# Two-layer encoder on one core: conditioning vector loaded as eight rows, inputs loaded first, layer 0's rotary tables made by TensorE

## The chip, the cores and the metric

One core of one Trainium2 chip. The kernel is written in Bass; its own planner simulates five engines (TensorE as PE, VectorE as DVE, ScalarE as ACT, GpSimd as POOL, and SyncE as SP, which issues every load) and writes the instructions in the order that the simulation gave. The metric is the device time of one launch in microseconds, lower is better.

## The reference

A two-layer encoder over 256 tokens of width 1024. Each layer has a mixer (grouped-query attention with normed and rotated queries and keys, a dilated windowed attention, gates) and a squared-ReLU MLP of width 4096. Both are preceded by an RMS norm that is scaled and shifted by numbers made from a vector c:

```python
c_act = jax.nn.silu(c)
for l in range(DEPTH):
    ada = c_act @ w_ada[l] + b_ada[l]
    sh1, sc1, gt1, sh2, sc2, gt2 = [a[:, None, :] for a in jnp.split(ada, 6, axis=-1)]
    h = rms(x, g_mix[l]) * (1.0 + sc1) + sh1
    parts = jnp.split(h @ w_in[l], IN_SPLITS, axis=-1)
    qa = axial_rope(rms(qa, q_norm_a[l]), row_cs, col_cs)      # likewise k, and apply_rope for branch B
    ...
    x = x + gt1 * (mixed @ w_out[l])
    h2 = rms(x, g_mlp[l]) * (1.0 + sc2) + sh2
    x = x + gt2 * (jnp.square(jax.nn.relu(h2 @ w_ff1[l])) @ w_ff2[l])
```

All arrays are fp32; every weight is read once, so 6 x 1024 x 1024 weights a layer go into `ada` alone.

## The kernel before, in words

**Precision and weights.** A product of fp32 matrices is made of three fp32r matmuls (`mm3`): both operands are split into a rounded part and the rest. A weight piece is a tile of 128 x 1024 (512 KB), loaded into one of six raw buffers (`wr`). ACT writes its rounded part and DVE the rest (`split_next`); the pair is called `w`. The activations are kept as such a pair too, `hT`.

**The dot products with c.** `ada` is no matmul: for each output block of 128 the transposed piece of w_ada is loaded into a raw buffer as well, and one DVE instruction multiplies it by c_act, which stands on all 128 partitions, and sums along the row (`ada_tile`). 96 such pieces cover both layers. The results of a norm are `shg` (shift and scale); `sh_sc` adds the bias and the norm's weights.

**The beginning.** SP loads c spread over 128 partitions (512 KB, of which each row is the same 4 KB), the two halves of x (each 128 tokens, 512 KB), the identity and the small tile. ACT and DVE make silu of c on the whole 128 x 1024 tile. For each half of x, ACT sums the squares (`sum_sq`), POOL takes the power -1/2, DVE scales, PE transposes against the identity, and ACT copies the result into `xT` (`rms_x`).

**The loop of layer 0's first projection.** Eight k steps. Each needs two pieces of w_ada (shift and scale for this block of 128), their small instructions (`sh_sc`), then h = xT times scale plus shift on ACT twice (once in fp32, once rounded into `hT`), the rest on DVE, and two weight pieces, w_x and w_y, of four chunks by two token halves: 24 matmuls of 512 columns into eight accumulators that fill all PSUM banks. So a step takes in four loads of 512 KB, and on DVE two dot products, two weight rests, one rest of hT and the factors.

**The rotary tables.** `rope_tables(l)` loads the constants (`cst`, 256 KB, once) and the norm weights of the heads spread over 128 partitions (`gains`, twice 256 KB), ACT multiplies half of the gains by 8, and POOL multiplies gains and cosines or sines, eight instructions. For layer 0 it is recorded at k step 3, for layer 1 at the end of layer 0's MLP. The tables are used by `qk_post`, after the loop.

**What sets the order.** `Plan.due` gives each instruction a due time, worked back from PE's sequence; `Plan.run` starts, on each engine, the ready instruction that is due first and whose buffers are free. All instructions are then issued from line 492, so the profile knows them by that line and by their tiles. SP issues loads strictly in its order: a load whose raw buffer is still being read holds up all loads behind it. The eight DMA semaphores go round, so a load also waits for the one eight places ahead of it.

## Time and profile before

| | us |
|---|---|
| median of three runs | 770.52 (769.89 to 770.74) |
| profiled execution | 770.36 |
| its span | 768.6 |
| PE busy | 736.4 (96%) |
| DVE busy | 583.3 (76%) |
| ACT busy | 445.4 (58%) |
| POOL busy | 104.4 (14%) |

The page gives, for each engine, busy time, share of the span and number of instructions. In an order of time each row has its start, its duration, engine, line, operation, output and inputs, and in brackets the idle time before it and what ended it. Several like instructions may be drawn together in a row (x24). In the views, `shg` are the factors of a norm, `ss` the sums of squares, `s2k` a scratch tile, `ps` a PSUM bank, `tabs` the rotary tables.

### The profile page before, as it was taken

To read this page: it belongs to the slowest core of one execution; us is meant where nothing else is said; L and a number is where in the kernel's file an instruction comes from. 1 tells how busy PE (TensorE), PEld (TensorE's weight loads), DVE (VectorE), ACT (ScalarE), POOL (GpSimd) and SP (SyncE) were. 2 spreads that over 40 slices of the span, in tenths; PEclk is the share of its full clock that TensorE was granted. 3 is DMA by queue.
4 is the path that set the end of the run, shared out by engine and by line. 5 is a ranking of instruction groups with operands and counts; after the bars stand their busy time and mean duration, and the time that the engine had idled before them with its cause. 6 is when DMAs were issued, how large, how long until landed. Compare 5 with 4: busy or idle time off the path is not lost.

```text
span 768.6 us, 12113 instructions
## 1 busy us (share of the span) xinstructions
PE 736.4 (96%) x4632; PEld 646.9 (84%) x4632; DVE 583.3 (76%) x846; ACT 445.4 (58%) x693; POOL 104.4 (14%) x88
## 2 busy tenths in 40 slices
PE   3899999999999999999999999999999999999997
PEld 2678787899778999988878888889987999988896
DVE  5899999998899989755387999855789975445512
ACT  6459549995246665555344655697734775545520
POOL 1307840000000006000013744000000000000000
PEclk9999999999999999999999999999999999999999
DMA  9895677895559999985423697943553996666201
GB/s 340 320 390 215 203 275 259 320 328 206 164 177 406 385 402 344 341 289 182 132 94 103 228 316 254 337 149 110 184 173 111 382 375 229 191 193 190 84 1 55
DMA packets 50666, 181.30 MB, mean 236 GB/s; under 512 B 5648, under 2 KB 5936, under 8 KB 50608
## 3 DMA queue, kind: packets, MB, share of 16 engines
q1 hardware_dynamic: 50608, 180.53, 66.6%
q8 instruction: 36, 0.59, 0.3%
q14 instruction: 22, 0.18, 0.1%
HBM read 179.44 MB, written 1.06 MB: 235 GB/s over the span
## 4 chain that ended last, share of the span: by engine, by line
PE 70%; DVE 19%; issue 5%; DMA 2%; ACT 2%; POOL 1%; SPq 0%; POOLq 0%; DVEq 0%
PE ps L492 70%; DVE s2k L492 10%; DVE w L492 6%; DMA ident<-in_ident 1%; DVE rstd L492 1%; DMA wr<-in_w_ada 1%; DVE hT L492 1%; ACT pr L492 1%; POOL ss L492 1%; DVE x L492 1%; DMA wr<-in_w_gate 1%; ACT w L492 1%; DVE st L492 0%; ACT s2k L492 0%; SPq L492 0%
## 5 line engine op out<-in xcount | busy, mean ns | idle before, releaser
L492 DVE TENSOR_TENSOR w<-wr,w 128x1024 fp32r<-128x1024 f32 x236 | 289.2, 1247 | 73.9 <-ACT w L492 73.3
L492 ACT ACTIVATE w<-wr 128x1024 fp32r<-128x1024 f32 x236 | 245.6, 1057 | 120.0 <-PE ps L492 57.9
L492 PE MATMUL ps<-hT,w 128*128 128x256 f32 x2112 | 270.4, 285 | 0.3 <-DVE w L492 0.3
L492 PEld LDWEIGHTS ps<-hT,w 128*128 128x128 f32 x2112 | 260.1, 191 | 7.0 <-issue 3.6
L492 PE MATMUL ps<-w,r2k 128*128 128x512 f32 x768 | 178.7, 392 | 0.0
L492 PEld LDWEIGHTS ps<-w,r2k 128*128 128x128 f32 x768 | 143.2, 188 | 30.5
L492 PE MATMUL ps<-w,hT 128*128 128x512 f32 x672 | 162.1, 395 | 5.4 <-ACT hT L492 3.6
L492 PEld LDWEIGHTS ps<-w,hT 128*128 128x128 f32 x672 | 123.8, 188 | 33.9 <-ACT hT L492 5.7
L492 DVE CUSTOM_DVE_ANT_0 s2k<-wr,c_act 128x1024 bf16<-128x1024 f32 x96 | 118.7, 1254 | 7.8 <-DMA wr<-in_w_ada 7.5
L492 ACT ACTIVATE s2k<-ps 128x512 f32<-128x512 f32 (+2 forms) x108 | 56.7, 558 | 69.5 <-PE ps L492 68.8
L492 POOL TENSOR_TENSOR ss<-ss,half 128x1 f32<-128x1 f32 x8 | 8.3, 1035 | 315.7 <-DVE ss L492 315.7
L492 POOL TENSOR_TENSOR s2k<-s2k,tabs 128x256 f32<-128x256 f32 (+1 forms) x40 | 39.5, 1009 | 84.7 <-DVE w L492 36.3
L492 DVE TENSOR_TENSOR r2k<-s2k,r2k 128x512 fp32r<-128x512 f32 x28 | 19.3, 689 | 36.5 <-ACT r2k L492 36.5
L492 PE MATMUL ps<-w,mT 128*128 128x512 f32 x192 | 44.5, 391 | 0.0
L492 PE MATMUL ps<-ident,s2k 128*128 128x128 f32 x148 | 23.7, 294 | 19.8 <-DMA ident<-in_ident 12.0
L492 PEld LDWEIGHTS ps<-w,mT 128*128 128x128 f32 x192 | 35.8, 188 | 7.3
L492 PEld LDWEIGHTS ps<-ident,s2k 128*128 128x128 f32 x148 | 18.0, 149 | 26.7 <-issue 13.4
L492 POOL TENSOR_TENSOR rstd<-rstd,half 128x8 f32<-128x8 f32 (+1 forms) x20 | 37.2, 1872 | 3.4 <-DVE rstd L492 3.1
L492 ACT ACTIVATE pr<-pr,st 128x256 f32<-128x256 f32 (+1 forms) x64 | 35.9, 614 | 1.8 <-DVE st L492 1.7
L492 ACT ACTIVATE s2k<-x 128x512 bf16<-128x512 f32 x16 | 10.0, 626 | 41.6 <-DVE x L492 41.6
L492 POOL TENSOR_TENSOR tabs<-s2k,cst 128x384 f32<-128x384 f32 (+1 forms) x16 | 19.9, 1281 | 76.8 <-ACT s2k L492 76.8
L492 DVE TENSOR_TENSOR s2k<-ps,gtb 128x512 f32<-128x512 f32 x16 | 11.0, 686 | 24.3 <-PE ps L492 24.3
(68 smaller groups left out, 472.7 us busy)
## 6 DMA issues: line engine op xcount, KB each, us to landing
wr<-in_w_ff SPq DMA_DIRECT2D x120, 512.0 KB, 5.0
wr<-in_w_ada SPq DMA_DIRECT2D x96, 512.0 KB, 5.1
wr<-in_w_gate SPq DMA_DIRECT2D x32, 512.0 KB, 5.1
wr<-in_w_qkv SPq DMA_DIRECT2D x24, 512.0 KB, 4.3
wr<-in_w_x SPq DMA_DIRECT2D x16, 512.0 KB, 4.4
wr<-in_w_out SPq DMA_DIRECT2D x16, 512.0 KB, 5.0
wr<-in_w_y SPq DMA_DIRECT2D x8, 512.0 KB, 5.5
wr<-in_w_ba SPq DMA_DIRECT2D x8, 512.0 KB, 4.5
```

Source lines behind the costliest of these rows:

```text
L492: getattr(self.real[o["e"]], o["op"])(*map(real, o["a"]), **{n: real(z) for n, z in o["k"].items()})
```

## The change

1. **c.** c is loaded as a tile of 8 x 128. ACT takes tanh of it, DVE one instruction (tanh + 1) * c, so that the tile holds twice the silu; the dot products are scaled by 0.5. PE then spreads the eight rows over 128 partitions: eight fp32 matmuls, each with one column of the identity, repeated 128 times, as the stationary operand over 8 rows. ACT copies the two banks into c_act.
2. **Loads first.** Loads recorded under `plan.first()` get a due time ahead of everything: c, x's first half, identity, x's second half, the small tile.
3. **Warm-up.** Three fp32 matmuls of a zeroed 128 x 512 tile into a bank that nobody reads stand at PE's beginning.
4. **Sum of squares.** That of x's second half in layer 0's first norm goes from ACT to DVE.
5. **Layer 0's tables.** The cosines and sines come transposed (`cs_t`, 64 head columns by 256 tokens, 256 KB), the norm weights of the heads as eight columns of the small tile. DVE makes, for both halves of the partitions, an identity of 64 times each of the eight columns (`diag`); a matmul over 64 rows then gives cos times gain in one go: per token half four matmuls (128 and 384 columns, cosines in the upper 64 rows of the array, sines in the lower), and ACT copies the two banks into the tables. POOL and the spread gains are out of layer 0. `cst` is loaded in `rope_tables`, now only for layer 1.
6. **The planner.** A price for fp32 matmuls of more than 256 columns over 128 rows, and caching that leaves its rules as they were.

```diff
+    def first(self):
+        self.soon = True
+        yield
+        self.soon = False
...
+            if o["soon"]:
+                due[i] = i - 1e9
...
-        dve.tensor_tensor_reduce(junk, raw, c_act, 1.0, 0.0, ALU.mult, ALU.add, col)
+        dve.tensor_tensor_reduce(junk, raw, c_act, 0.5, 0.0, ALU.mult, ALU.add, col)
...
-        if CFG["dve_ss"]:
+        if (l, w, t) == (0, 0, 1):
             dve.tensor_tensor_reduce(junk, xc, xc, 1.0 / D, 0.0, ALU.mult, ALU.add, o)
...
+    def first_tables():
+        tabs = tl("sbuf", [P, 2, 2, 8, HD], F32, "b8", NB8, "tabs0")
+        cs = s2k("cs").rearrange("p (o n) -> p o n", o=2)
+        sp.dma_start(cs, a["cs_t"])
+        gc = small[:, 128:136]
+        dve.tensor_scalar(gc[:, 1::2], gc[:, 1::2], 8.0, None, op0=ALU.mult)
+        e = s2k("eye")[:, :HD]
+        dve.tensor_tensor(e, ident[:, 0:HD], ident[:, HD:P], op=ALU.add)
+        dg = s2k("diag")
+        dve.tensor_tensor(
+            dg.rearrange("p (s n) -> p s n", s=8), e[:, None, :].to_broadcast([P, 8, HD]),
+            gc[:, :, None].to_broadcast([P, 8, HD]), op=ALU.mult,
+        )
+        for t in range(2):
+            pss = [pt(f"tab{t}{hf}") for hf in range(2)]
+            with plan.together():
+                for o, (s0, s1) in enumerate(((0, 2), (2, 8))):
+                    for hf in range(2):
+                        rows = slice(HD * hf, HD * (hf + 1))
+                        pe.matmul(
+                            pss[hf][:, s0 * HD : s1 * HD], cs[rows, o, t * P : (t + 1) * P],
+                            dg[rows, s0 * HD : s1 * HD], start=True, stop=True,
+                        )
+            for hf in range(2):
+                act.activation(tabs[:, t, hf], pss[hf].rearrange("p (s n) -> p s n", s=8), AF.Copy)
+        return tabs
...
     def rope_tables(l):
+        sp.dma_start(cst, a["cst"])
...
-    sp.dma_start(c_act, a["c"].partition_broadcast(P))
-    for t in range(2):
-        sp.dma_start(x[:, t, :], a["x"][t])
-    sp.dma_start(ident, a["ident"])
-    sp.dma_start(small, a["small"])
-    c_sig = tl("sbuf", [P, 2 * D], F32, "b8", NB8, "c_sig")[:, :D]
-    act.activation(c_sig, c_act, AF.Tanh, scale=0.5)
-    act.activation(c_sig, c_sig, AF.Copy, scale=0.5, bias=0.5)
-    dve.tensor_tensor(c_act, c_act, c_sig, op=ALU.mult)
+    c_row = cp.tile([KT, P], F32, name="c_row")
+    with plan.first():
+        sp.dma_start(c_row, a["c"])
+        for t in range(2):
+            sp.dma_start(x[:, t, :], a["x"][t])
+            if t == 0:
+                sp.dma_start(ident, a["ident"])
+        sp.dma_start(small, a["small"])
+    c_sig = s2k("c_sig")[:KT, :P]
+    act.activation(c_sig, c_row, AF.Tanh, scale=0.5)
+    dve.scalar_tensor_tensor(c_row, c_sig, 1.0, c_row, op0=ALU.add, op1=ALU.mult)
+    warm = tl("sbuf", [P, 2 * D], F32, "b8", NB8, "warm")[:, :512]
+    dve.memset(warm, 0.0)
+    cold = tl("psum", [P, 512], F32, "ps", 8, "cold")
+    for _ in range(WARM):
+        pe.matmul(cold, warm[:, :P], warm, start=True, stop=True)
+    for g in range(2):
+        ps = pt(f"c{g}")
+        for k in range(4):
+            kk = 4 * g + k
+            pe.matmul(
+                ps[:, k * P : (k + 1) * P], ident[:KT, kk : kk + 1].to_broadcast([KT, P]), c_row,
+                start=True, stop=True,
+            )
+        act.activation(c_act[:, g * 512 : (g + 1) * 512], ps, AF.Copy)
...
+    tabs_of[0] = first_tables()
     hT = h_tiles(0, 0)
...
         if k == 3:
-            sp.dma_start(cst, a["cst"])
             sp.dma_start(mask, a["mask"])
-            tabs_of[0] = rope_tables(0)
```

**How the instructions move.** The beginning differs, the loop, and a few places of the qk post-processing behind it; from there on the engines run through the same rows, but for the late load of `cst` and one weight rest on DVE. First SP at the beginning of the program, before and now (`wr` are the raw buffers):

```order
L492 DMA c_act<-in_c 128x1024
L492 DMA x<-in_x 128x1024 x2
L492 DMA wr_99<-in_w_ada 128x1024
L492 DMA wr_100<-in_w_ada 128x1024
L492 DMA wr_101<-in_w_x 128x1024
L492 DMA ident<-in_ident 128x128
L492 DMA small<-in_small 128x128
L492 DMA wr_102<-in_w_y 128x1024
L492 DMA wr_103<-in_w_ada 128x1024
L492 DMA wr_104<-in_w_ada 128x1024
L492 DMA s2k_79<-in_gains 128x512
L492 DMA cst<-in_cst 128x512
```

```order
L523 DMA c_row<-in_c 8x128
L523 DMA x<-in_x 128x1024
L523 DMA ident<-in_ident 128x128
L523 DMA x<-in_x 128x1024
L523 DMA small<-in_small 128x136
L523 DMA wr_101<-in_w_ada 128x1024
L523 DMA wr_102<-in_w_ada 128x1024
L523 DMA s2k_74<-in_cs_t 128x512
L523 DMA wr_103<-in_w_x 128x1024
L523 DMA wr_104<-in_w_y 128x1024
L523 DMA wr_105<-in_w_ada 128x1024
L523 DMA wr_106<-in_w_ada 128x1024
```

x, the identity and the small tile stand ahead of all weights; the spread c, both gains and `cst` are gone from here, `cs_t` is new.

Then DVE at its beginning, before, and now from its sums of squares of x's second half to the first dot product with c (an ISA row with `wr` and `c_act` is a dot product, one with `x` a sum of squares, one without inputs reads out the sum; `small` holds the gains):

```order
L492 MEMSET half 128x16
L492 TENSOR_TENSOR c_act<-c_act,c_sig 128x1024
L492 SCALAR_TENSOR_TENSOR ss_75<-ss_75 128x1
L492 ISA s2k_85,shg_96<-wr_99,c_act 128x1024
L492 ISA shg_96 128x1
L492 TENSOR_SCALAR s2k_81<-x,ss_75 128x512
L492 ISA s2k_82,shg_96<-wr_100,c_act 128x1024
L492 ISA shg_96 128x1
```

```order
L523 ISA s2k_79,ss_92<-x 128x512
L523 ISA ss_92 128x1
L523 ISA s2k_80,ss_92<-x 128x512
L523 ISA ss_92 128x1
L523 TENSOR_SCALAR s2k_75<-x,ss_91 128x512
L523 SCALAR_TENSOR_TENSOR ss_92<-ss_92 128x1
L523 TENSOR_SCALAR s2k_76<-x,ss_91 128x512
L523 TENSOR_SCALAR small<-small 128x4
L523 TENSOR_TENSOR s2k_78<-s2k_77,small 128x512
L523 TENSOR_SCALAR s2k_79<-x,ss_92 128x512
L523 TENSOR_SCALAR s2k_80<-x,ss_92 128x512
L523 ISA s2k_75,shg_98<-wr_101,c_act 128x1024
```

The first dot product stood fourth and stands seventeenth now, behind two sums of squares, the four scalings of x, the scaling of small and the diagonal (`s2k_78`). Last, DVE between step 0's rest of `hT` and step 1's, before and now (`w` are the weights' rests, read from a raw buffer):

```order
L492 TENSOR_TENSOR hT_95<-s2k_82,hT_94 128x256
L492 ISA s2k_81,shg_96<-wr_103,c_act 128x1024
L492 ISA shg_96 128x1
L492 ISA s2k_83,shg_96<-wr_104,c_act 128x1024
L492 ISA shg_96 128x1
L492 TENSOR_TENSOR shg_96<-shg_96,small 128x2
L492 SCALAR_TENSOR_TENSOR shg_96<-shg_96,small 128x1
L492 TENSOR_TENSOR w_107<-wr_99,w_107 128x1024
L492 TENSOR_TENSOR hT_95<-s2k_84,hT_94 128x256
```

```order
L523 TENSOR_TENSOR hT_97<-s2k_76,hT_96 128x256
L523 ISA s2k_79,shg_98<-wr_105,c_act 128x1024
L523 ISA shg_98 128x1
L523 TENSOR_TENSOR w_108<-wr_104,w_108 128x1024
L523 ISA s2k_80,shg_98<-wr_106,c_act 128x1024
L523 ISA shg_98 128x1
L523 TENSOR_TENSOR shg_98<-shg_98,small 128x2
L523 SCALAR_TENSOR_TENSOR shg_98<-shg_98,small 128x1
L523 TENSOR_TENSOR w_109<-wr_101,w_109 128x1024
L523 TENSOR_TENSOR w_110<-wr_102,w_110 128x1024
L523 TENSOR_TENSOR hT_97<-s2k_75,hT_96 128x256
```

The second weight rest of step 0 (`w_108` now) and both of step 1 stand between the two rests of `hT` now, where one weight rest stood. On ACT the four copies into the tables stand behind step 0's two weight pieces and ahead of step 1's. On PE the three warm-ups, the eight matmuls that spread c, the sixteen transposes and the eight matmuls of the tables stand ahead of step 0, in this order.

More of the change, by code (lines that the diff above doesn't have):

```diff
@@ L2 @@
 from contextlib import ExitStack, contextmanager, nullcontext
+from functools import lru_cache
 import ml_dtypes
@@ L40 @@
 NB8 = 14
+WARM = 3
 QA, KA, VA, B0, GA = 0, 512, 640, 768, 3072
@@ L162, in together @@
     @contextmanager
+    def first(self):
+        self.soon = True
+        yield
+        self.soon = False
+    @contextmanager
     def together(self):
@@ L180, in foot, with blocks @@
         p0, at = divmod(x.offset, row)
+        return name, str(x.space), p0, p0 + parts, Plan.blocks(at, tuple(map(tuple, dims[1:])), size, row)
+    @staticmethod
+    @lru_cache(None)
+    def blocks(at, dims, size, row):
         idx = np.array([at])
-        for step, n in dims[1:]:
+        for step, n in dims:
             if step:
@@ L188, in foot @@
             m |= 1 << b
-        return name, str(x.space), p0, p0 + parts, m
+        return m
     def record(self, e, op, a, k):
@@ L197, in record @@
         o = dict(e=e, op=op, a=a, k=k, w=[self.foot(z) for z in outs], r=[self.foot(z) for z in ins], i=len(self.ops))
-        o["also"], o["then"] = [], None
+        o["also"], o["then"], o["soon"] = [], None, self.soon and e == "SP"
         if self.group is not None:
@@ L214, in cost @@
             if op == "matmul" and F32R not in (ins[0].dtype, ins[1].dtype):
+                if n > 256 and ins[0].ap[0][1] == P:
+                    return 1.7 * n, 1.7 * n + 220.0
                 return 1.0 * n, n + 220.0
@@ L349, in run @@
         then = dict.fromkeys(ORDERED)
+        state = [0]
+        seen = dict.fromkeys(ORDERED)
         def fits(i):
             more = {}
-            for name in sorted((z for z in names_of[i] if z not in begun), key=lambda z: place[z]):
+            new = [z for z in names_of[i] if z not in begun]
+            if not new:
+                return True
+            for name in sorted(new, key=lambda z: place[z]):
                 tag = self.tiles[name]
@@ L386, in run @@
                     heapq.heappush(q, (due[i], i))
+                    seen[e] = None
+                if pick is None and seen[e] == state[0]:
+                    continue
                 held = []
@@ L396, in run @@
                         break
+                if pick is None:
+                    seen[e] = state[0]
                 if pick is not None and e != "SP" and not forced:
@@ L432, in run @@
                     live[tag] += 1
+                    state[0] += 1
                     begun.add(name)
@@ L453, in run @@
                         if not users[name]:
+                            state[0] += 1
                             live[self.tiles[name]] -= 1
@@ L527, in encoder @@
     x = cp.tile([P, 2, D], F32, name="x")
-    small = cp.tile([P, 96 + 32], F32, name="small")
+    small = cp.tile([P, 96 + 32 + 8], F32, name="small")
     c_act = cp.tile([P, D], F32, name="c_act")
@@ L1264, in _constants @@
     mask = np.where(np.stack(rows, 1), 0.0, NEG).astype(ml_dtypes.bfloat16)
-    return cst, mask, np.eye(P, dtype=np.float32)
+    cs_t = np.ascontiguousarray(cst.transpose(3, 4, 2, 1, 0)).reshape(P, 2, S)
+    return cst, cs_t, mask, np.eye(P, dtype=np.float32)
 def _layout(i):
@@ L1273, in _layout @@
     r["x"] = con(f["x"].reshape(16, 4, 4, D).transpose(2, 1, 0, 3)).reshape(2, P, D)
-    r["c"] = f["c"].reshape(D)
+    r["c"] = f["c"].reshape(KT, P)
     b = f["b_ada"].reshape(2, 2, 3, KT, P)
@@ L1277, in _layout @@
     g = np.stack([f["g_mix"], f["g_mlp"]], 1).reshape(2, 2, KT, P).transpose(3, 0, 1, 2).reshape(P, 32)
-    r["small"] = con(np.concatenate([b_col, g], 1))
     r["w_ada"] = con(f["w_ada"].transpose(0, 2, 1)).reshape(2, 2, 3, KT, P, D)
@@ L1285, in _layout @@
     r["gains"] = con(np.stack([gains, sw], 1).reshape(2, 2, 512))
+    g0 = r["gains"][0].reshape(2, 8, HD).transpose(0, 2, 1).reshape(P, 8)
+    r["small"] = con(np.concatenate([b_col, g, g0], 1))
     cc = _chunk_cols()
@@ L1304, in _layout @@
     r["w_ff2"] = con(f["w_ff2"].reshape(2, 32, P, 1024))
-    r["cst"], r["mask"], r["ident"] = _constants()
+    r["cst"], r["cs_t"], r["mask"], r["ident"] = _constants()
     return r
```

## Prediction

> **What bounds the kernel now.** I read the page first, then who TensorE (PE) waits for, then PE's own order of time, then the engines that feed it, at the start. On the page:
>
> ```profile
> span 768.6 us, 12113 instructions
> PE 736.4 (96%) x4632; PEld 646.9 (84%) x4632; DVE 583.3 (76%) x846; ACT 445.4 (58%) x693; POOL 104.4 (14%) x88
> ```
>
> PE is busy for 736.4 of 768.6 us, so the change can win only from the 32 us in which it is not. PE's waits over the whole span:
>
> ```profile
> PE ps L492 <- DMA ident<-in_ident: 12.0, 1, 12.0
> PE ps L492 <- DVE s2k L492: 7.2, 10, 1.8
> PE ps L492 <- ACT hT L492: 3.6, 5, 1.2
> ```
>
> The 12.0 us lie ahead of PE's first instruction; the 3.6 lie in layer 0's first projection, eight k steps of 24 matmuls. PE in order of time:
>
> ```profile
> 12.02 3.65 PE L492 MATMUL ps<-ident,s2k 128*128 128x128 f32 x16 [12.02 <-DMA ident<-in_ident]
> 16.62 5.76 PE L492 MATMUL ps<-w,hT 128*128 128x512 f32 x24 [0.96 <-ACT hT L492]
> 23.56 1.19 PE L492 MATMUL ps<-w,hT 128*128 128x512 f32 x4 [1.18 <-ACT hT L492]
> 25.49 4.83 PE L492 MATMUL ps<-w,hT 128*128 128x512 f32 x20 [0.74 <-DVE hT L492]
> 30.70 5.76 PE L492 MATMUL ps<-w,hT 128*128 128x512 f32 x24 [0.37 <-ACT hT L492]
> 36.66 5.74 PE L492 MATMUL ps<-w,hT 128*128 128x512 f32 x24 [0.20 <-ACT hT L492]
> 43.28 22.08 PE L492 MATMUL ps<-w,hT 128*128 128x512 f32 x96 [0.89 <-ACT hT L492]
> 65.20 0.99 PE L492 MATMUL ps<-hT,w 128*128 128x256 f32 x7
> ```
>
> From step 4 on PE runs without a gap: 96 matmuls from 43.28 to 65.20, 0.228 us each, **5.48 us a step**. Eight such steps are 43.8 us; the loop takes 65.20 - 16.62 = 48.6. So 4.8 us are lost inside it, nearly all in steps 1 to 3, and 16.62 before it. The end of this loop, 65.20, is the number that the change must move. What made step 1 late is on VectorE (DVE) and GpSimd (POOL):
>
> ```profile
> 12.69 0.16 DVE L492 SCALAR_TENSOR_TENSOR shg<-shg,small 128x1 f32<-128x1 f32 x1
> 16.95 1.22 DVE L492 CUSTOM_DVE_ANT_0 s2k<-wr,c_act 128x1024 bf16<-128x1024 f32 x1
> 18.09 2.03 DVE L492 CUSTOM_DVE_ANT_0 s2k<-wr,c_act 128x1024 bf16<-128x1024 f32 x1
> 21.05 0.38 DVE L492 SCALAR_TENSOR_TENSOR shg<-shg,small 128x1 f32<-128x1 f32 x1
> 23.05 1.79 DVE L492 TENSOR_TENSOR w<-wr,w 128x1024 fp32r<-128x1024 f32 x1 [1.62 <-ACT w L492]
> 17.92 7.83 POOL L492 TENSOR_TENSOR tabs<-s2k,cst 128x384 f32<-128x384 f32 x8 [4.92 <-ACT s2k L492]
> ```
>
> While POOL builds the rotary tables (17.92 to 25.75), the same DVE instruction takes 2.03 us instead of 1.22, and a one-column one 0.38 instead of 0.16. Undisturbed, DVE's long instructions follow each other by 1.14 us (16.95 to 18.09).
>
> **Part by part: the start.** ScalarE (ACT), DMA and DVE up to step 0, with two later rows of DVE:
>
> ```profile
> 0.74 0.39 SPq L492 DMA_DIRECT2D c_act<-in_c  x1
> 1.18 0.89 SPq L492 DMA_DIRECT2D x<-in_x  x2
> 5.30 1.06 ACT L492 ACTIVATE c_sig<-c_act 128x1024 f32<-128x1024 f32 x1 [3.29 <-DMA c_act<-in_c]
> 14.85 0.60 ACT L492 ACTIVATE xT<-ps 128x512 f32<-128x512 f32 x1 [0.16 <-PE ps L492]
> 15.48 0.60 ACT L492 ACTIVATE s2k<-xT,shg 128x256 f32<-128x256 f32 x1
> 15.99 0.58 ACT L492 ACTIVATE hT<-xT,shg 128x256 fp32r<-128x256 f32 x1
> DMA to landing us min/median/max: 5.5/5.9/6.3
> 0.81 0.07 DVE L492 MEMSET half<- 128x16 f32 x1 [0.81 <-PEq L1313]
> 7.47 1.22 DVE L492 TENSOR_TENSOR c_act<-c_act,c_sig 128x1024 f32<-128x1024 f32 x1 [6.59 <-ACT c_sig L492]
> 13.04 0.88 DVE L492 TENSOR_SCALAR s2k<-x,ss 128x512 f32<-128x512 f32 x2 [0.18 <-POOL ss L492]
> 47.80 0.42 DVE L492 TENSOR_TENSOR hT<-s2k,hT 128x256 fp32r<-128x256 f32 x1
> 53.25 0.43 DVE L492 TENSOR_TENSOR hT<-s2k,hT 128x256 fp32r<-128x256 f32 x1
> ```
>
> Step 0's factors were ready on DVE at 12.69 + 0.16 = 12.85, yet ACT used them at 15.48: its queue stood behind the copies of the transposes, and these behind the identity. That cover goes; what is late next is DVE's chain:
>
> - Loads. The first 512 KB (c) were usable at 5.30, 4.6 us after issue; x's halves landed 5.5 and 6.3 us after their issues at 1.18 and about 1.6, so at 6.7 and 7.9. Now x's first half is the first big load: 5.3 at the latest (if the slow beginning is the queue's, not c's), 4.3 if it runs as x did. One 512 KB load costs 1.25 us (7.9 - 6.7), the identity's 64 KB an eighth. I take 5.3: identity 5.5, x's second half 6.7.
> - DVE, from 6.7: two sums of squares of 512 columns (half of 1.14 each) 1.2; four scalings of x, 0.44 each, 1.8; the diagonal, a 512-column instruction, 0.6; small ones 0.3; two dot products 2.3; the factors 0.4. That ends at **13.3**, 0.45 later than before: DVE got some 2.5 us of new work in front (sums of squares, diagonal, memset, identity's halves) and lost the 1.22 of c's product. POOL's power for x's second half (its row waits 0.18 for it above) lies beside a scaling and the diagonal. Without a row for the sums of squares' short form I bound them by 0.44 each (a scaling) and 0.7 (over half of 1.22): 13.0 to 13.5.
> - c comes off this path: it is spread by eight fp32 matmuls of 128 columns (0.22 each by the row below, 0.43 at half clock: 1.7 to 3.4 us) after the identity and the warm-ups, and two ACT copies of 0.6; over between 8.5 and 11, and DVE reads it at 10.6. ACT gives up two passes over c (1.06 each) and two squares.
> - PE's tables stand in front of step 0. fp32 prices and the full clock:
>
> ```profile
> 78.02 0.60 PE L492 MATMUL ps<-ident,s2k 128*128 128x128 f32 x4
> 111.73 1.13 PE L492 MATMUL ps<-ka,qk 64*128 64x256 f32 x8
> L492 PE MATMUL ps<-ident,s2k x148: 270/273/445, 12.0 to 597.0; 128*128 128x128 f32 x148
> ```
>
> One matmul lasts 0.27 us, overlapping the next. Four transposes take 0.60, so they start 0.11 apart; the first 16 took 3.65, 0.21 apart: half rate. The second row is four fp32 products of 64 rows, two by two in the halves of the array: (1.13 - 0.27) / 2 = 0.43 per pair of 256 columns, so 0.22 per pair of 128 and 0.65 per pair of 384: 1.7 us for all eight table matmuls if they run side by side, 3.5 if not. Transposes end near 11.5 (x's last scaling 10.6), tables at 13.2 or 15.0. I take 13.2, since their operands lie in the same halves as that row's. The warm-ups (three fp32 products of 512 columns: 2.6 us at full rate, 5.1 at half) run from about 1.5, behind DVE's memset that starts where the one at 0.81 did, while only loads are under way.
> - So ACT starts step 0's h at 13.3, and PE at 13.3 + (16.62 - 15.48) = **14.45**, where it was 16.62: 2.2 earlier. The other end, tables not side by side, is 15.0.
>
> **The loop.** Between its step-0 and step-1 rests of hT, DVE now has five long instructions (three weight rests, two dot products). A step with four took 53.25 - 47.80 = 5.45, so 0.89 of it is short work (factors, hT's rest of about 0.35), and five make 6.6. The step-0 rest ends at 13.3 + 1.14 + 0.35 = 14.8, so step 1's at 21.4. PE ends step 0 at 19.9, has 0.7 us of matmuls that need only the rounded part, and so step 1 counts from 20.7 and ends at 26.2; before, step 2 began at 30.70. POOL's 7.83 us are gone, ACT pays four copies of tables (0.6 each) after step 0's weights, before step 1's, and they end by 17.5, ahead of PE's need of those banks. Step 2's rest needs three long instructions, 4.3: 25.7. Later steps cost DVE 5.45 at most, less than PE's 5.48, so from 26.2 PE sets the pace: six steps, **59.1 against 65.20: 6.1 us**.
>
> The loads have to keep up:
>
> ```profile
> 16.60:23.50 6.90, 5.76 (x24) 4.43 (x24) 5.21 (x8) 3.69 (x8) 5.58 (x6) 1.00 1.03 419
> 23.50:30.70 7.20, 6.03 (x25) 4.35 (x25) 7.12 (x11) 4.17 (x6) 2.25 (x3) 1.00 0.71 241
> 48.00:54.00 6.00, 6.00 (x28) 4.99 (x27) 5.91 (x11) 3.66 (x5) 0.00 (x0) 1.00 1.02 406
> 280.00:290.00 10.00, 10.00 (x55) 8.63 (x55) 7.62 (x10) 4.90 (x8) 2.14 (x2) 1.00 1.03 394
> ```
>
> (Columns: window, length, PE, PEld, DVE, ACT, POOL busy, clock, DMA share, GB/s.) A step eats four loads, 2.1 MB in 5.48 us: 383 GB/s, under the 419 and 406 shown. Up to the last weights of the loop 18.5 MB go: 44 us at 419, from about 2 on; they land near 47.5 and are needed at 56. The Trainium skill (DMA: Bandwidth & Descriptors, Specifications) puts a core's HBM limit at about 358 GB/s; by that the last weights land near 55, are split by 57.2, and the loop ends near 60, a gain of 5.2. The rows, above 358 for windows on end, contradict it.
>
> The rotary constants, 256 KB, are now loaded a second time, in a stretch where DMA is full (the last row). PE has no gap there, and weights are split well ahead; I cost it at nothing, and at 0.65 us (256 KB at 394 GB/s) if the cover failed.
>
> Behind the loop the same instructions follow in nearly the same order, so the shift stays: 768.6 - 6.1 = 762.5 of span. The profiled execution took 770.36, 1.8 more than its span and 0.16 below the median of 770.52. Forecast: **764.4**.
>
> **Rivals.** (1) The load buffers' turn stays the limit in steps 2 and 3, as the 241 GB/s window suggests: a load goes out only when DVE has read an old one. Those steps then take the 5.96 and 6.62 of before (30.70, 36.66, 43.28), 1.6 more than forecast: 766.0. Against it: the window lies right behind POOL's disturbance. 16%. (2) PE's clock falls back between the spread of c and step 0, where only transposes keep it awake for some 3 us; step 0 then begins at half rate, and 3.4 us at half rate cost 1.7: 766.1. Against it: after nothing but 16 transposes, step 0 took 5.76 at 16.62, as step 2 did at 30.70, so transposes had raised the clock. The Trainium skill (TensorE: Matmul & The Clock Gate, PE-mode transpose) states the rule of this rival, that transposes don't count as PE activity; the trace disagrees. 10%. (3) More: DVE, no longer held up, runs further ahead of PE by the loop's end than the 0.6 of before, and of PE's waits for it behind the loop (the longest 1.8) up to 1.5 goes: 762.9. Against it: the load buffers tie it to PE. 12%. (4) Nothing: the post-processing behind the loop is DVE's and takes back what PE won: 770.5. Against it: that work can begin only when the loop's banks are done, so it moves along. 3%. (5) Slower: PE stays at half clock through all that now stands ahead of step 0, because zeros and 8-row products don't wake it. Warm-ups 5.1, c 3.4, transposes 3.4, tables 6.9: from 1.5 to 20.3; step 0 at half rate 10.3, ending at 30.6, and seven steps more end at 69.0, 3.8 behind: 774.3. It decides if the clock is still half at about 26. Against it: the before's 3.65 us of transposes were enough. 4%.
>
> **The numbers.** The forecast's case has 55%; its own range is 763.3 (x lands 1 us sooner) to 765.6 (tables not side by side, cover of the late load gone). With rivals 1 to 3 that is 93%, and the range 762.3 to 767.0 holds all four with some room beside their prices. A measurement tells 0.2% (1.5 us) from no change: faster 0.93, same 0.03, slower 0.04.
>
> **What would show it.** Right: PE's first transposes near 8 to 9, step 0 near 14.5, DVE's dot products at 1.2 us throughout, PE gapless from about 26, the 256-column matmuls beginning near 59. Wrong: matmuls of step 0 at twice their time (2, 5); DVE waiting on DMA in steps 2 to 4 (1); x's second half later than 7.5; a loop end near 59 with a span above 766, which would mean the gain is given back behind it.

## The result and the profile after

The changed kernel takes **765.22 us** (median of four runs, 764.64 to 766.63) against 770.20 us for the kernel before beside it (769.69 to 770.74): a ratio of 0.9938, interval 0.9921 to 0.9955, or 5.0 us. The profiled execution took 765.02 us with a span of 763.2, 5.4 less than the 768.6 of before. The forecast was 764.4.

The page of the changed kernel, with the same columns as before:

```profile
span 763.2 us, 12186 instructions
PE 744.3 (98%) x4670; PEld 651.8 (85%) x4670; DVE 583.7 (76%) x854; ACT 443.8 (58%) x692; POOL 92.8 (12%) x80
```

TensorE is busy 7.9 us longer (warm-ups, spread, tables), though the whole is shorter. Whom TensorE waits for (total, times, longest):

```profile
PE ps L523 <- DVE s2k L523: 9.3, 12, 1.8
```

The 12.0 us for the identity and the 3.6 for `hT` are gone; the waits for VectorE's `s2k` have grown from 7.2 to 9.3. TensorE in order of time:

```profile
6.87 2.29 PE L523 MATMUL ps<-c_row,ident 8*128 8x128 f32 x16
9.08 1.09 PE L523 MATMUL ps<-ident,s2k 128*128 128x128 f32 x8
10.45 1.67 PE L523 MATMUL ps<-ident,s2k 128*128 128x128 f32 x8 [0.28 <-DVE s2k L523]
12.05 3.05 PE L523 MATMUL ps<-s2k,s2k 64*128 64x128 f32 x16
15.03 44.36 PE L523 MATMUL ps<-w,hT 128*128 128x512 f32 x192
59.23 0.51 PE L523 MATMUL ps<-hT,w 128*128 128x256 f32 x3
61.34 0.30 PE L523 MATMUL ps<-ident,s2k 128*128 128x128 f32 x1 [1.61 <-DVE s2k L523]
```

Step 0 begins at 15.03 (before: 16.62), all 192 matmuls of the loop run as one block, and it ends at 59.23 (65.20). The first 128 x 128 transposes behind the loop, those of the keys, wait 1.61 us for VectorE where they waited 0.31 before (66.50):

```profile
66.50 0.30 PE L492 MATMUL ps<-ident,s2k 128*128 128x128 f32 x1 [0.31 <-DVE s2k L492]
```

VectorE at the start and in step 3, and its last rest of `hT`:

```profile
7.02 0.69 DVE L523 CUSTOM_DVE_ANT_0 s2k<-x 128x512 bf16<-128x512 f32 x1 [1.11 <-DMA x<-in_x]
9.30 0.69 DVE L523 TENSOR_TENSOR s2k<-s2k,small 128x512 f32<-128x512 f32 x1
10.71 1.22 DVE L523 CUSTOM_DVE_ANT_0 s2k<-wr,c_act 128x1024 bf16<-128x1024 f32 x1
13.31 0.16 DVE L523 SCALAR_TENSOR_TENSOR shg<-shg,small 128x1 f32<-128x1 f32 x1
14.69 0.43 DVE L523 TENSOR_TENSOR hT<-s2k,hT 128x256 fp32r<-128x256 f32 x1
...
30.38 1.23 DVE L523 TENSOR_TENSOR w<-wr,w 128x1024 fp32r<-128x1024 f32 x1 [0.74 <-ACT w L523]
...
53.27 0.43 DVE L523 TENSOR_TENSOR hT<-s2k,hT 128x256 fp32r<-128x256 f32 x1
```

From its first dot product at 10.71 VectorE has hardly a gap up to step 7's rest at 53.27; the largest is the 0.74 in step 3, where a weight landed late. Before, its rests of step 0 and step 7 were:

```profile
16.60 0.43 DVE L492 TENSOR_TENSOR hT<-s2k,hT 128x256 fp32r<-128x256 f32 x1 [0.42 <-ACT hT L492]
58.65 0.43 DVE L492 TENSOR_TENSOR hT<-s2k,hT 128x256 fp32r<-128x256 f32 x1
```

### The profile page after: what moved, and what is told of

Read it like the earlier page. It is cut to its first block, busy times and chain, and to the rows that moved or that the text cites. A ratio compares the mean times of both kernels' runs of the same rounds, so it can differ in the third digit from the quotient of the medians.

```text
span 763.2 us, 12186 instructions
## 1 busy us (share of the span) xinstructions
PE 744.3 (98%) x4670; PEld 651.8 (85%) x4670; DVE 583.7 (76%) x854; ACT 443.8 (58%) x692; POOL 92.8 (12%) x80
## 4 chain that ended last, share of the span: by engine, by line
PE 70%; DVE 19%; issue 5%; DMA 2%; ACT 2%; POOL 1%; POOLq 0%; SPq 0%; DVEq 0%; ACTq 0%
PE ps L523 70%; DVE s2k L523 9%; DVE w L523 6%; DVE rstd L523 1%; DMA wr<-in_w_x 1%; DMA wr<-in_w_gate 1%; ACT pr L523 1%; POOL ss L523 1%; DMA x<-in_x 1%; DVE x L523 1%; ACT w L523 1%; DVE hT L523 1%; ACT s2k L523 0%; DVE st L523 0%; DVE shg L523 0%
## 5 line engine op out<-in xcount | busy, mean ns | idle before, releaser
L523 ACT ACTIVATE qk<-ps 128x512 f32<-128x512 f32 x16 | 9.6, 598 | 29.9 <-PE ps L523 29.9
```

Source lines behind the costliest of these rows:

```text
L523: getattr(self.real[o["e"]], o["op"])(*map(real, o["a"]), **{n: real(z) for n, z in o["k"].items()})
```

## The experiments

The theory at this point had two halves: VectorE, freed of GpSimd, feeds TensorE sooner; and TensorE's earlier loop end carries through. The rival was that the earlier start alone, or the clock, did it. In each expectation the letters mean what it says there. In the diffs `...` stands for lines left out, among them those that keep the planner's order where the text says that it is kept. All kernels were timed against the kernel before in the same batch (769.62, 769.97, 770.15 and 770.09 us in the four batches). The table has the marks that turned out to matter, from each kernel's profile (one execution), and the median and ratio of all its runs. A ratio's interval reaches 0.0009 to 0.0017 (about 1 us) to either side, so smaller differences between two kernels are not told apart by their totals:

| run | PE step 0 | DVE rest, step 0 | DVE rest, step 7 | key transposes | span | span less step-7 rest | median | ratio to before, interval |
|---|---|---|---|---|---|---|---|---|
| before | 16.62 | 16.60 | 58.65 | 66.50 | 768.6 | 710.0 | 770.20 | |
| changed | 15.03 | 14.69 | 53.27 | 61.34 | 763.2 | 709.9 | 765.22 | 0.9938 (0.9921 to 0.9955) |
| changed again | 14.76 | 14.74 | 52.52 | 60.60 | 762.2 | 709.7 | 765.67 | 0.9940 (0.9927 to 0.9953) |
| tables on GpSimd | 16.09 | 16.06 | 58.11 | 66.19 | 769.1 | 711.0 | 772.01 | 1.0037 (1.0023 to 1.0051) |
| only the tables | 17.10 | 17.08 | 56.19 | 64.27 | 765.8 | 709.6 | 767.63 | 0.9971 (0.9962 to 0.9981) |
| squares on ScalarE | 16.50 | 15.88 | 53.86 | 61.94 | 764.1 | 710.2 | 766.43 | 0.9957 (0.9944 to 0.9969) |
| later transposes | 14.88 | 14.54 | 52.61 | 61.15 | 762.2 | 709.6 | 764.49 | 0.9937 (0.9924 to 0.9949) |
| no warm-up | 14.54 | 14.52 | 53.01 | 61.10 | 762.4 | 709.4 | 764.87 | 0.9939 (0.9925 to 0.9952) |
| spread of 128 rows | 14.93 | 14.91 | 52.79 | 60.87 | 762.5 | 709.7 | 764.89 | 0.9934 (0.9922 to 0.9946) |
| GpSimd beside | 15.49 | 15.47 | 60.22 | 68.31 | 771.1 | 710.9 | 771.09 | 1.0013 (1.0004 to 1.0022) |
| TensorE later | 16.71 | 14.95 | 53.35 | 61.62 | 764.0 | 710.7 | 765.56 | 0.9941 (0.9929 to 0.9954) |
| VectorE later | 14.98 | 14.96 | 54.50 | 62.58 | 766.3 | 711.8 | 766.00 | 0.9951 (0.9939 to 0.9964) |
| shorter VectorE chain | 16.80 | 16.78 | 56.42 | 64.50 | 766.9 | 710.5 | 766.82 | 0.9954 (0.9941 to 0.9968) |
| mask later | 15.45 | 15.12 | 53.18 | 61.25 | 762.9 | 709.7 | 764.97 | 0.9941 (0.9926 to 0.9956) |

**The two halves of the change apart.** First the changed kernel with layer 0's tables back on GpSimd:

```diff
-    tabs_of[0] = first_tables()
...
         if k == 3:
+            tabs_of[0] = rope_tables(0)
```

> Layer 0's tables go back to POOL with their three 256 KB loads; c as eight rows, loads first, warm-ups and the squares on DVE stay. Theory A (the gain is the lead that DVE wins in the loop, and POOL's tables took 2.8 us of it): DVE's dot products and weight rests of steps 1 and 2 reach 1.5 to 2.0 us again, step 7's rest of hT comes 2 to 3 us later than in the changed kernel (53.3), time 767.2 to 768.2. Rival B (the loads and the early start of step 0 make the gain, POOL is hidden): step 0 at 14 to 14.5, since tables and diagonal are gone from in front of it, time 764.5 to 765.5.

Both numbers missed: at 772.01 it is slower than the kernel before. Its TensorE:

```profile
12.30 2.82 PE L523 MATMUL ps<-ident,s2k 128*128 128x128 f32 x12 [2.98 <-DVE s2k L523]
16.09 13.06 PE L523 MATMUL ps<-w,hT 128*128 128x512 f32 x48 [0.96 <-ACT hT L523]
30.27 33.87 PE L523 MATMUL ps<-w,hT 128*128 128x512 f32 x144 [1.12 <-ACT hT L523]
```

TensorE waits 2.98 us between the transposes, and steps 0 and 1, 48 matmuls, take 13.06 us instead of 10.96: by the trace's clock record the clock is half from 9.86 to 20.1. GpSimd works from 18.33 on for 8.07 us, beside VectorE as before. From step 0's to step 7's rest VectorE needs 42.05 us, exactly what it needed before; by then only 0.54 us are won, and 1.0 is lost behind the loop, where the planner's order is another one. The half clock cost nothing inside the loop that the rows show: ScalarE's h of step 2 waits 2.71 us for VectorE's factors (row at 29.12), and TensorE then waits 1.12 for that step's `hT`. Ahead of step 0 it slowed the transposes from 12.30 on; what that cost isn't separated. (This profile was the shortest of the kernel's runs, 770.85.)

Then the other half, the kernel before with the tables on TensorE and nothing else changed:

```diff
+    tabs_of[0] = first_tables()
...
         if k == 3:
-            tabs_of[0] = rope_tables(0)
```

> The kernel before with only the tables on PE: c still comes spread (512 KB) and is multiplied on all partitions, no warm-up, squares on ACT, no rule that loads go first (the planner now draws x and the identity ahead by itself, since tables and transposes are due early). Theory A: most of the gain is here, since POOL is off and the identity is early; step 0 at 15.5 to 16, loop without waits on DVE, time 766 to 767. Rival B: the 512 KB of c and the second pass over it keep step 0 at 16.5, time 768 to 769.5.

It falls between the two theories: 767.63. Step 0 is later than before (17.10; the tables wait 1.7 us for `cs_t`, and half of them run at half clock), but VectorE needs 39.11 us between the two rests instead of 42.05. So without GpSimd VectorE gains 2.9 us between the rests, and the kernel 2.0 against the 769.62 beside it; the other half alone loses 2.4, and both together gain 5.0: the parts don't add up.

**GpSimd's price by itself.** The changed kernel, all orders kept, with eight products of 128 x 384 on GpSimd, whose result nobody reads, where the kernel before had its eight:

```diff
...
+    for i in range(8):
+        pool.tensor_tensor(dump, tabs_of[0][:, i // 4, i // 2 % 2, :6].rearrange("p s n -> p (s n)"),
+            tabs_of[0][:, i // 4, i // 2 % 2, 2:].rearrange("p s n -> p (s n)"), op=ALU.mult)
...
```

> The changed kernel with GpSimd given eight products of 128 x 384 (tables times tables, into a tile that nobody reads) from about 16 to 24 us, in the place where the kernel before had its eight; everything else, order included, stays, so this adds only GpSimd's work beside VectorE. Theory A (the gain was VectorE freed from GpSimd): dot products and weight rests in that window take about 2.0 us instead of 1.2, step 1's rest of hT comes 2 to 3.5 us later (23 to 24.7), PE waits for it, loop end 61.5 to 63, total 2 to 3.5 us above the changed kernel. Rival B (the kernel that had its tables on GpSimd again lost its time by TensorE's half clock at step 0): VectorE catches up inside PE's slack, total at most 0.7 us above the changed kernel.

771.09: 5.4 us more than the changed kernel's 765.67 in the same batch, more than theory A allowed and far from B. GpSimd and VectorE side by side:

```profile
16.95 12.96 POOL L525 TENSOR_TENSOR dump<-tabs 128x384 f32<-128x384 f32 x8 [6.57 <-ACT tabs L525]
```

```profile
16.95 2.08 DVE L525 TENSOR_TENSOR w<-wr,w 128x1024 fp32r<-128x1024 f32 x1
18.96 2.03 DVE L525 CUSTOM_DVE_ANT_0 s2k<-wr,c_act 128x1024 bf16<-128x1024 f32 x1
21.04 0.85 DVE L525 TENSOR_TENSOR shg<-shg,small 128x2 f32<-128x2 f32 x1
22.00 3.96 DVE L525 TENSOR_TENSOR w<-wr,w 128x1024 fp32r<-128x1024 f32 x2
25.88 1.21 DVE L525 TENSOR_TENSOR hT<-s2k,hT 128x256 fp32r<-128x256 f32 x1
27.02 2.02 DVE L525 CUSTOM_DVE_ANT_0 s2k<-wr,c_act 128x1024 bf16<-128x1024 f32 x1
28.97 2.02 DVE L525 CUSTOM_DVE_ANT_0 s2k<-wr,c_act 128x1024 bf16<-128x1024 f32 x1
```

Eight products, and eight VectorE instructions with two inputs that last 0.7 to 0.9 us longer than usual (1.22, 0.16 and 0.43), whether they have 1024 columns or two: 6.3 us. (A ninth in that stretch, of one column at 21.92, took its usual 0.16.) The products are held up in turn: 12.96 us for eight instead of 7.83. In the kernel before VectorE stood idle for 1.62 us beside them, and only 2.8 us were lost (its rows 2.03, 0.85, 0.38, 1.79, 0.67 and 1.48 against the usual 1.22, 0.16, 0.16, 1.23, 0.43 and 1.22). So the price was more than double where VectorE had no gaps. It is not what made the first half of the change worth nothing: with the tables on GpSimd VectorE's rows between 18.69 and 27.48 (0.97, 0.93, 0.92, two instructions in 3.33, and 1.48) are 3.3 us longer than usual, little more than before. The rest was lost in a step 0 whose rest came at 16.06 instead of 14.69, since the dot products stood ahead of x's last scalings there and the transposes ran at half clock, and in 1.17 us of waiting for `hT` at 21.79. The Trainium skill (SBUF — State Buffer, SBUF: two separate sides) says that a GpSimd instruction and a VectorE instruction with two SBUF inputs take the shared ports in turn, each for its whole length, and do not split the bandwidth; these rows agree for eight of the nine.

**Who sets the end of the loop?** In all rows of the table but three (before, 7.85; later transposes; TensorE later, 8.27) the key transposes begin 8.07 to 8.09 us behind VectorE's step-7 rest, whatever TensorE's loop end was, and 709.4 to 711.8 us are left from that rest to the end, though the rest itself moves by 7.7. Two kernels tell VectorE from TensorE. One delays TensorE alone, by two fp32 matmuls ahead of step 0, which step 0 overwrites:

```diff
+                    if k == 0 and pair == (0, 1) and i == 0 and t == 0:
...
+                        for _ in range(2):
+                            pe.matmul(pss[c][t], ident, x[:, 0, :512], start=True, stop=True)
...
                     mm3(pss[c][t], lh, ll, wh, wl, k == 0, k == KT - 1)
```

> The changed kernel with two more fp32 matmuls of 512 columns (identity times x, into a bank that step 0's first product overwrites) on TensorE between the tables and step 0, about 1.8 us; all else keeps its order. Theory P (the prediction's: the total goes as TensorE's loop end, the shift stays): loop end 1.3 to 1.7 later than 59.2, total 1.3 to 1.7 us above the changed kernel. Theory D (VectorE sets it: in all runs so far the first key transposes begin 8.08 us after VectorE's step-7 rest of hT, and 709.4 to 711 us are left from that rest to the end): the rest stays at 52.5 to 53.3, TensorE's loop ends 1.3 to 1.7 later, but its wait for the first key transposes, 0.9 to 1.6 us, shrinks by as much; total at most 0.5 us above the changed kernel.

Its TensorE:

```profile
16.71 44.12 PE L532 MATMUL ps<-w,hT 128*128 128x512 f32 x192
60.66 0.51 PE L532 MATMUL ps<-hT,w 128*128 128x256 f32 x3
61.62 0.31 PE L532 MATMUL ps<-ident,s2k 128*128 128x128 f32 x1 [0.45 <-ACT s2k L532]
```

Step 0 begins 2 us later than in the second profile of the changed kernel (14.76), the loop ends 1.5 us later (60.66 against 59.19), and the total is the same: 765.56 (0.9941) against 765.67 (0.9940). The wait ahead of the transposes, 0.9 to 1.6 us in the changed kernel, has absorbed most of it: against the first profile, whose step-7 rest is nearest (53.27 to 53.35), the loop ends 1.43 us later and the transposes begin 0.28 later. P's smallest 1.3 us stands at the edge of what the intervals of the totals exclude, so the marks weigh more here than the totals. The other delays VectorE alone, by three products behind step 5's rest that nobody reads:

```diff
+        if k == 5:
...
+            for _ in range(3):
+                dve.tensor_tensor(dump, f32(hT[1][:, k, :]), f32(hT[0][:, k, :]), op=ALU.mult)
```

> The changed kernel with three more products of 128 x 256 on VectorE (step 5's rest of hT times its rounded part, into a tile that nobody reads), 1.0 to 1.1 us, right behind step 5's rest of hT; all else keeps its order. Theory P: TensorE runs gapless and has its weights ahead, so its loop end stays at 59.0 to 59.4 and the total is within 0.3 us of the changed kernel. Theory D: VectorE runs without a gap, so its step-7 rest of hT comes 1.0 to 1.1 us later (53.6 to 54.3), the first key transposes too (61.7 to 62.4, TensorE waiting 2 us or more there), and the total is 0.9 to 1.2 us above the changed kernel.

Its VectorE, then its TensorE:

```profile
42.77 1.34 DVE L532 TENSOR_TENSOR dump<-hT,hT 128x256 f32<-128x256 f32 x3
49.09 0.43 DVE L532 TENSOR_TENSOR hT<-s2k,hT 128x256 fp32r<-128x256 f32 x1
54.50 0.43 DVE L532 TENSOR_TENSOR hT<-s2k,hT 128x256 fp32r<-128x256 f32 x1
```

```profile
60.36 0.51 PE L532 MATMUL ps<-hT,w 128*128 128x256 f32 x3
62.58 0.30 PE L532 MATMUL ps<-ident,s2k 128*128 128x128 f32 x1 [1.70 <-DVE s2k L532]
498.79 0.33 PE L532 MATMUL ps<-ident,pr 128*128 128x128 f32 x1 [0.98 <-ACT pr L532]
```

The rest comes 1.2 to 2.0 us later than in the two profiles of the changed kernel (54.50 against 53.27 and 52.52), the transposes 1.2 to 2.0, and TensorE's loop too (60.36): its last steps depend on VectorE, which P denied. The marks say D. The median moves by 0.3 to 0.8 us (766.00 against 765.67 and 765.22) and the ratio by 0.8 (0.9951 against 0.9940), less than D's 0.9 to 1.2, and the intervals overlap; so D's place is shown, its full size in the total isn't. This profile was the longest of the kernel's runs (768.04), in part for a reason far behind: a wait of 0.98 at 498.79 that the profiles of the changed kernel lack at that place.

The view that follows the work that ended last back to its causes says the same of the two kernels compared here: in the one before, from 16.60 on to the first key transposes, and in the changed one over the whole loop, the chain runs over rows of VectorE and ScalarE and the loads that they wait for, and no matmul of the loop is in it.

**What is given back behind the loop.** In the changed kernel the first key transposes stand behind three gate matmuls where seven stood before. This kernel puts them behind 18 and the next behind 42, on TensorE alone:

```diff
...
+        for t, n in ((0, 18), (1, 42)):
+            tp = start[outs[f"qT0_1_{t}"][0]]
+            for i in outs["g0_0"][:n]:
+                if start[i] > tp:
+                    at[i] = tp - 1e-3
```

> The changed kernel, but behind the loop the two transposes of the first key chunk stand after 18 and 42 of the first gate's matmuls instead of 3 and 34; all other engines keep their rows. Theory A (behind the loop DVE sets the pace, so PE's waits of 1.61 and 0.74 cost nothing of their own): those two waits go, later waits on DVE grow by as much, time 764.9 to 765.5. Rival D (the order that the planner chose there gives back what PE had won, 5.97 at the loop's end against 5.4 at the end): 1 to 1.8 us faster, 763.4 to 764.2.

```profile
61.15 0.27 PE L533 MATMUL ps<-ident,s2k 128*128 128x128 f32 x1
...
65.44 0.30 PE L533 MATMUL ps<-ident,s2k 128*128 128x128 f32 x1 [1.16 <-DVE s2k L533]
...
71.12 0.63 PE L533 MATMUL ps<-ident,s2k 128*128 128x128 f32 x4 [1.23 <-DVE s2k L533]
```

The first wait is gone, the second is 1.16 instead of 0.74, the third 1.23 instead of 0.30: VectorE's pace stands behind all of them. The median, 764.49, lies between A's range and D's; the ratio, 0.9937, is that of the changed kernel, so no gain is shown.

**The clock ahead of step 0.** In the changed kernel the granted clock is full from 7.40, half from 10.81 and full from 14.23 (clock record), so the tables take 3.05 us. Two kernels ask why, and whether it costs anything. One spreads c from a tile of 128 rows, of which 120 are zero, with the same eight matmuls:

```diff
+    c_pad = cp.tile([P, P], F32, name="c_pad")
+    dve.memset(c_pad, 0.0)
...
-                ps[:, k * P : (k + 1) * P], ident[:KT, kk : kk + 1].to_broadcast([KT, P]), c_row,
+                ps[:, k * P : (k + 1) * P], ident[:, kk : kk + 1].to_broadcast([P, P]), c_pad,
```

> The changed kernel with c's eight rows in a tile of 128 rows, the others zero, so that the spread is made by the same eight matmuls over 128 rows instead of 8; all orders stay. Theory R (what counts for the clock is the share of the array's rows: 8 of 128 let it fall): the clock stays full from the warm-ups into step 0, tables take 1.7 to 2.0 us instead of 3.05, step 0 at 14.4 to 14.6, total 0.3 to 0.7 us below the changed kernel. Rival G (what let it fall is PE's idle time between the transposes, or anything else in that window): the clock falls as before, tables 3 us or so, step 0 at 14.9 to 15.2, total as the changed kernel's.

```profile
5.95 1.95 PE L523 MATMUL ps<-c_pad,ident 128*128 128x128 f32 x16
9.08 1.09 PE L523 MATMUL ps<-ident,s2k 128*128 128x128 f32 x8 [1.18 <-DVE ss L523]
10.66 1.09 PE L523 MATMUL ps<-ident,s2k 128*128 128x128 f32 x8 [0.48 <-DVE s2k L523]
11.68 2.01 PE L523 MATMUL ps<-s2k,s2k 64*128 64x128 f32 x16
14.93 6.73 PE L523 MATMUL ps<-w,hT 128*128 128x512 f32 x27 [1.24 <-ACT hT L523]
```

The clock stays full from 5.15 to the end, the tables take 2.01, and step 0 begins no sooner: TensorE now waits 1.24 us for `hT`, for which VectorE's factors are late. Theory R holds for the clock, not for step 0; the total lies below the control's by what R said (0.9934 against 0.9940), but the intervals overlap, so a gain isn't shown. The other takes the three warm-ups out:

```diff
-WARM = 3
+WARM = 0
```

> The changed kernel without its three warm-up matmuls; all orders stay. Theory W (the warm-ups buy a full clock for the spread of c, no more, and the clock falls back anyway): the spread takes 3.4 to 4.6 us instead of 2.3 but begins earlier, since no warm-up stands ahead of it; transposes at half rate, tables at full or half rate as the window falls; step 0 at 14.6 to 15.6, total within 0.6 us of the changed kernel. Rival V (without warm-ups PE stays at half clock up to step 0 and into it): step 0 at 15.5 or later and at 0.46 us a matmul for up to 3.4 us, total 1 to 2.5 us above the changed kernel.

```profile
4.95 3.75 PE L523 MATMUL ps<-c_row,ident 8*128 8x128 f32 x16 [4.95 <-DMA ident<-in_ident]
8.64 3.66 PE L523 MATMUL ps<-ident,s2k 128*128 128x128 f32 x16
12.23 2.06 PE L523 MATMUL ps<-s2k,s2k 64*128 64x128 f32 x16
14.54 6.73 PE L523 MATMUL ps<-w,hT 128*128 128x512 f32 x27 [0.25 <-ACT hT L523]
```

Spread and transposes run at half rate, the tables at full, and 764.87 (0.9939) is the changed kernel's time: W. The warm-ups do nothing for the total that these runs can tell.

**The control**, the changed kernel once more:

> The changed kernel once more, as a control for the kernels beside it: 0.992 to 0.996 of the kernel before. If the phase of the clock's windows against the kernel's start is free, the start differs a little from the first profile (tables 1.7 to 3.5 us, step 0 between 14.3 and 15.6) while everything behind it keeps its distances.

0.9940, and the clock's windows lie otherwise (full from 5.31, half from 8.73, full from 12.14): the tables take 2.01, step 0 begins at 14.76.

**Attempts to shorten VectorE's chain.** First the squares of x's second half back on ScalarE:

```diff
-        if (l, w, t) == (0, 0, 1):
+        if (l, w, t) == None:
```

> The changed kernel with the squares of x's second half back on ACT, which is idle from 5.6 to 8.3 us; DVE has 1.2 us less in front of step 0. Theory A (DVE's chain in front of step 0 sets the lead): step 0's factors 0.7 to 1.2 us earlier than 13.47, step 0 near 14.2, step 7's rest of hT at 52.3 to 52.8, time 764.2 to 764.6. Rival C (the loads set the pace in steps 2 to 4): DVE waits longer for w_x there, step 7's rest stays at 53.3, time 765.0 to 765.4.

766.43, slower than either expected. The planner now puts half of the tables ahead of the second transposes on TensorE, all of it at half clock (2.08 for eight records where 1.14 is usual), and step 0's `hT` waits for the last transposes: VectorE's step-0 rest comes at 15.88. A second attempt added the spread of 128 rows and loaded the small tile ahead of x's second half, so that the diagonal is ready early:

```diff
             if t == 0:
                 sp.dma_start(ident, a["ident"])
-        sp.dma_start(small, a["small"])
+                sp.dma_start(small, a["small"])
```

> The changed kernel with the spread over 128 rows (TensorE's clock stays full), both sums of squares of x's second half back on ScalarE, and the small tile loaded ahead of x's second half, so that the diagonal is made while VectorE waits for x: some 1.9 us less on VectorE between x's landing and step 0's factors, of which waits for c's spread and for the first piece of w_ada may give back one. Theory D: step 0's factors 0.6 to 1.3 us sooner than in the run with the spread over 128 rows alone, step-7 rest of hT at 51.5 to 52.3, total 0.5 to 1.2 us below it (ratio 0.992 to 0.9935). Theory P: step 0 on TensorE starts sooner by as much, and the total follows too; the two part where TensorE is late for another reason (the transposes behind the tables): then P gives no gain.

766.82. The clock is full, but the tables stand ahead of the second transposes again, and there they wait for their constants:

```profile
12.43 1.14 PE L523 MATMUL ps<-s2k,s2k 64*128 64x128 f32 x8 [2.63 <-DMA s2k<-in_cs_t]
13.50 1.09 PE L523 MATMUL ps<-ident,s2k 128*128 128x128 f32 x8
```

In this profile x's second half came 2 us later than in the changed kernel (ScalarE took it up at 9.20, VectorE there at 7.02); why, stays open. Last, the mask's load (256 KB), which stands in the loop's busiest stretch, moved eighteen loads on, with the spread of 128 rows kept:

```diff
...
+        at[sps[k][1]] = sps[k + 18][0] + 1e-3
```

> The changed kernel with the spread over 128 rows (TensorE's clock stays full up to step 0) and the mask's load (256 KB, needed only behind the loop) moved from step 3 eighteen loads later, behind the loop's last weights. Theory L (VectorE sets the pace, 5.41 us a step when nothing is late, and what it loses beside, 0.5 to 0.8 us once in most profiles, is a weight that lands late because the mask stands in the loads' queue): no step beyond 5.5 us, step-7 rest of hT 37.8 us behind step 0's, 52.3 to 52.8, total 763.8 to 764.8, a ratio of 0.992 to 0.9935. Rival M (late weights come of the load buffers' turn or of the memory's own swings, the mask has no part in it): one step of 5.9 to 6.1 us stays in the profile, or the profile is like that of the run with the spread over 128 rows alone, total 764.6 to 765.6.

764.97, a ratio of 0.9941: no gain. One step of 5.70 us remains (a late weight, 0.32 us), so M is nearer, but some profiles lose a different half microsecond behind the mask's place, and this one didn't. Whether the mask has a part in such late weights stays open. No version beats the changed kernel by more than the interval.

## Why the prediction was right, step by step

- **The start on VectorE: right.** x's second half was there at 7.02 (6.7 forecast), the two sums of squares took 1.23 us (1.2), the diagonal 0.61 (0.6), the factors were ready at 13.31 + 0.16 = 13.47 (13.3).
- **TensorE's step 0 at 14.45: 0.6 short.** The table matmuls lie side by side, 2.0 us at full clock (1.7 forecast), but the forecast took the full clock, and here most of them ran at half: 3.05. That is rival 2's mechanism, which did come true, at a fraction of its price, since the clock opened before step 0. It isn't the whole 0.6: in the control, with tables of 2.01, TensorE waited for `hT` and began at 14.76. It cost nothing in the end: TensorE 1.5 us later still gave the same total.
- **The loop: right.** The rests of steps 1 and 2 came at 21.13 and 25.39 (21.4 and 25.7), the end at 59.23 (59.1). Step 0's 0.6 did not move the end, since the forecast had TensorE wait 0.8 ahead of step 1 (19.9 to 20.7), and that wait took it up. Rival 1 shows in small, 0.74 us in step 3: that weight's load went out at 22.73, when a dot product had freed its buffer, and landed 6.5 us later.
- **The loads: right in the outcome, not in the margin.** The forecast had the loop's last weights land near 47.5; the last w_x went out at 45.19, landed 5.3 us later, and ScalarE waited 1.77 us for it. VectorE frees the buffers, so the loads keep its pace and do not run ahead at full bandwidth. The slowest windows of the loop (GB/s last in the row) still moved 363 and 356, and VectorE lost 0.74 us to one late weight there:

```profile
26.00:32.00 6.00, 6.00 (x29) 4.94 (x28) 5.19 (x10) 3.02 (x5) 0.00 (x0) 1.00 1.01 363
32.00:38.00 6.00, 6.00 (x28) 4.97 (x27) 5.86 (x10) 3.40 (x5) 0.00 (x0) 1.00 0.97 356
```

- **The late load of `cst`: right.** It is issued at 278.1, and TensorE has no gap between 275 and 300.
- **"The shift stays": the step that failed.** TensorE's lead of 5.97 us at the loop's end was 5.16 at the key transposes and 5.4 at the end. The forecast put the end of the loop on TensorE ("from 26.2 PE sets the pace"). With 5.45 us a step at most (it took 5.41) against TensorE's 5.48 VectorE seemed to have slack; but behind the loop its post-processing is next, in the order of its own queue, and the transposes wait for that. VectorE's lead at step 7 was 58.65 - 53.27 = 5.38, and that is what the span got. The number that the change had to move was VectorE's last rest, not 65.20. The two differ by 0.6 us here, so the total came out right: that it lies 0.8 us from the forecast and not further is luck as far as this step goes. The kernel with TensorE later shows how far the step could have led astray: 1.5 us at the loop's end were worth nothing there. Rival 3 let the waits behind the loop shrink; the first of them grew from 0.31 to 1.61.
- **Rival 5, slower** by a clock that stays at half, lies one edit away: with the tables on GpSimd the clock was at half until 20.1 and the total above the kernel before. But the half clock cost nothing inside the loop there, as said above, and the kernel without warm-ups, at half clock up to 12.37, was as fast as the changed one; so rival 5's price is not seen. (Its own sum has 10.3 for a step 0 at half rate, where twice 5.48 is 11.0.)

The 5.4 us are thus 1.9 from the earlier start (VectorE's step-0 rest, 16.60 to 14.69) and 3.5 from the time between the two rests (42.05 to 38.58), of which 2.9 were seen with the tables alone. In the control's profile, without the late weight, the time between the rests is 37.78.

## What to carry to other kernels

When the busiest engine runs without gaps behind another one that is nearly as full, follow the fed engine's first wait *behind* the stretch: whoever ends that wait sets the kernel's pace, and only its lead is kept. Work that shares VectorE's ports is priced by how full VectorE is at that moment, so an edit that fills VectorE's gaps makes GpSimd's work beside it dearer (2.8 us with gaps, 6.3 without, for eight products of the same size). Gains that do not add up (2.0 and a loss of 2.4 apart, 5.0 together) have to be costed together. An earlier start on TensorE buys nothing while VectorE's chain is what the first step waits for.

## What the runs showed of the hardware

- GpSimd's elementwise products and VectorE's two-input instructions alternate: 0.7 to 0.9 us more on each of eight VectorE instructions, even on one of two columns (0.16 to 0.85); one of a single column between them was not held up (0.16).
- The clock is granted by windows of 3.41 us whose place against the kernel's start changes from run to run (first full at 4.35 to 7.42 with the same warm-ups). A window with warm-ups' end and an 8-row spread was followed by a half one, and the same with 128 rows by a full one (windows from 5.31 and from 5.15). The clock also fell behind waiting: in the run with the mask moved, with 128 rows and 1.8 us of waiting, at 11.18; with GpSimd beside, at 27.02 within 2.9 us of waiting. But the second attempt to shorten VectorE's chain waited 2.63 us, across two windows, and kept the full clock, so how much waiting it takes isn't shown.
- Transposes raise the clock: without warm-ups, 16 of them and the 8-row spread were all but the first 0.14 us of the tables that stood before the full clock at 12.37. The Trainium skill (TensorE: Matmul & The Clock Gate, PE-mode transpose) says that they don't count as activity; this trace disagrees, as that of the kernel before did.
- The view by windows writes a clock of 1.00 where the trace has no clock record (in the kernel without warm-ups up to 12 us); there the matmuls' own durations tell the rate.
